# The first products of a two-layer encoder: a new order, small matmuls of zeros ahead of x, and two squares moved back

## The chip, the cores and the metric

The kernel runs on one core of one Trainium2 chip. A core has five engines with a queue each, worked off in order: TensorE (PE in the profile, its weight loads PEld), VectorE (DVE), ScalarE (ACT), GpSimd (POOL) and SyncE (SP, which here only issues transfers). They wait for one another through semaphores. The metric is the device time of one execution in microseconds (us); lower is better.

## The reference

Two layers, each of them: half of a SwiGLU feed-forward, a mixer (convolution, pooling, differential attention), half of a second feed-forward, and a norm. Input and output are 256 tokens of 1024 channels in float32. What is near the change is the start of the first layer:

```python
x = x + 0.5 * swiglu_ffn(rms_norm(x, ffn1_norm[l]), ffn1_w_gate[l], ffn1_w_up[l], ffn1_w_down[l])

def rms_norm(x, g):
    y = xf * lax.rsqrt(jnp.mean(xf * xf, axis=-1, keepdims=True) + NORM_EPS)
    return (y * g.astype(jnp.float32)).astype(x.dtype)

def swiglu_ffn(h, w_gate, w_up, w_down):
    return (jax.nn.silu(h @ w_gate) * (h @ w_up)) @ w_down
```

D_MODEL is 1024 and D_FF is 2816.

## The kernel before

Every matmul of the reference is made of fast single-pass products: each operand is split into a high part (`whi`, rounded by ScalarE) and a low part (`wlo`, the rest, by VectorE), and a product is high by high plus the cross terms. For the feed-forward's first two matrices `mm2` does this with two instructions: 512 columns against the high weights and 256 columns against the low weights. Such a pair is called a pair below.

x stands in four tiles `x[t][c]`: t is the half of the tokens, c the half of the channels, so x00 and x10 hold the first 512 channels and x01 and x11 the second. `Norm.chunk(c)` transposes one half of the channels on TensorE against an identity matrix (it stands in the first 128 columns of `cst`), splits the result into `n0a_xT0` to `n0a_xT3` (or 4 to 7), and sums the squares of x on ScalarE (`n0a_sq`). `Norm.factor` makes the norm's factor of these sums (`n0a_m` on VectorE, `n0a_r` on GpSimd) and spreads it with two TensorE transposes (`n0a_bc`) and a ScalarE copy (`n0a_rbc`). The factor is multiplied in after the products, so products need only the transposed x.

Weights come as 158 pieces of 1 MB through a queue on SyncE: `raw7a` and `raw7b` are the two halves of piece 7, and there are five half-piece buffers. Each piece is split in quarters: `whi7a` to `whi7d` on ScalarE, `wlo7a` to `wlo7d` on VectorE. A half-piece buffer is free when VectorE has made the low parts of it, and only then can SyncE issue the next transfer into it. The first piece comes in four quarters, and x01 and x11 are issued between them. The feed-forward `f0a` uses one piece for each of 22 blocks: block j accumulates the gate product `f0a_g` and the up product `f0a_u` over eight xT in two PSUM banks, of which four are in turn, so block j+2 can begin when ScalarE and VectorE have read block j's banks (`f0a_t`: a copy on ScalarE, then an addition on VectorE).

The order of the instructions is not that of the code. All calls are first recorded as operations with a cost and a lag (`_cost`, in us), and `Program.schedule` plans them: backwards for priorities, forwards to an order, four times, and keeps the shortest plan. `emit` then issues them all from line 429 in that order, so nearly every row of the profile names L429. Costs only set the order: on the chip an engine waits for its semaphores.

The planner prices a float32 matmul like this:

```python
        single = kw["rhs"].tile.dt == F32R
        return (n / 2400 + 0.0135 if single else max(4 * n / 2400 + 0.005, 0.215)), None, 0.0
```

After the first feed-forward has begun, `load_rest` brings the other 1 MB of `cst` through GpSimd's queue, once a buffer is free that TensorE reads.

Of the kernel before, what the change touches and what calls it, by code (L numbers as in the profile page):

```python
# [16 lines left out]
P = 128  # L17
# [38 lines left out]
ROUNDS = 4  # L56
IN_ORDER = ("mm", "raw")
# [152 lines left out]
class Program:  # L210
# [5 lines left out]
    def __init__(self, tc, nc):  # L216
        self.tc, self.nc = tc, nc
        self.ops = []
        self.open = None
        self.chains = {}  # L220
        self.waits = []
        self.after = set()
        for e in ("tensor", "vector", "scalar", "gpsimd", "sync"):
            setattr(self, e, _Engine(self, e))
# [14 lines left out]
    def add(self, engine, call, cost, reads, writes, table, lag):  # L239
        i = len(self.ops)  # L240
        if self.open is None or self.open == "new":
            op = Op()
            op.engine, op.cost, op.calls, op.preds, op.succs, op.tiles = engine, 0.0, [], set(), [], []
            op.table, op.lag = table, lag
            self.ops.append(op)
            if self.open == "new":
                self.open = op
        else:
            op = self.open
            i -= 1  # L250
            assert op.engine == engine
        op.calls.append(call)
# [240 lines left out]
def trunk_kernel(  # L493
# [11 lines left out]
    nc = Program(tc, tc.nc)  # L505
# [43 lines left out]
    cst = cpool.tile([P, P + NH * 384 + 512], F32, tag="cst", name="cst")  # L549
    nc.scalar.dma_start(cst[:, :P], consts[:, :P])  # L550
# [3 lines left out]
    def load_x(c):  # L554
        for t in range(2):
            nc.sync.dma_start(x[t][c], x_in[t * P:(t + 1) * P, c * 512:(c + 1) * 512])
# [22 lines left out]
    upad = cpool.tile([P, 2, SEQ + 2 * PPAD], F32, tag="upad", name="upad")  # L579
    for z in zpad:  # L580
        nc.gpsimd.memset(z, 0.0)
    nc.gpsimd.memset(upad, 0.0)

# [16 lines left out]
    class Norm:  # L600
# [9 lines left out]
        def chunk(self, c):  # L610
            name = self.name
            for kp in range(2):
# [6 lines left out]
                for j in range(2):  # L619
                    k = c * 4 + kp * 2 + j  # L620
                    s = slab_tile(f"{name}_xT{k}")
                    split(s[:, :256], s[:, 256:], tr[:, j * 256:(j + 1) * 256], self.gains[:, k:k + 1])
                    self.xT[k] = (s[:, :256], s[:, 256:])
                    self.xw[k] = s
            for t in range(2):
                sq = tmp.tile([P, 512], F32, tag="sq", name=f"{name}_sq{c}{t}")
                nc.scalar.activation(sq, x[t][c], AF.Square, scale=1.0 / 32.0, accum_out=self.ss[:, t, c:c + 1])
                if self.post is not None:
                    nc.vector.tensor_mul(x[t][c], x[t][c], self.post[:, c * 512:(c + 1) * 512])
                    sq = tmp.tile([P, 512], F32, tag="sq", name=f"{name}_sqg{c}{t}")  # L630
                    nc.scalar.activation(sq, x[t][c], AF.Square, scale=1.0 / 32.0, accum_out=self.ssg[:, t, c:c + 1])

# [348 lines left out]
    for c in range(2):  # L981
        norm.chunk(c)
# [167 lines left out]
```

## Time and profile before

| | us |
|---|---|
| median of three runs | 954.4 |
| the three runs | 954.4, 959.36, 953.64 |
| the profiled execution's own time | 956.96 |
| its span, from the first to the last instruction | 955.2 |

The profiled execution's time is 1.76 us more than its span, which is what lies around the instructions. All times below are from the start of the span. A row of the timeline gives start and duration; matmuls overlap, so the pace of equal neighbours is read from start to start, or from n of them as the duration of the row less that of one, over n - 1. Granted clock is the share of TensorE's 2.4 GHz: 1.00 is that, and 0.50 is 1.2 GHz.

### The profile page before, as it was taken

To read this page: it belongs to the slowest core of one execution; us is meant where nothing else is said; L and a number is where in the kernel's file an instruction comes from. 1 tells how busy PE (TensorE), PEld (TensorE's weight loads), DVE (VectorE), ACT (ScalarE), POOL (GpSimd) and SP (SyncE) were. 2 spreads that over 40 slices of the span, in tenths; PEclk is the share of its full clock that TensorE was granted. 3 is DMA by queue.
4 is the path that set the end of the run, shared out by engine and by line. 5 is a ranking of instruction groups with operands and counts; after the bars stand their busy time and mean duration, and the time that the engine had idled before them with its cause. 6 is when DMAs were issued, how large, how long until landed. Compare 5 with 4: busy or idle time off the path is not lost.

```text
span 955.2 us, 14812 instructions
## 1 busy us (share of the span) xinstructions
PE 934.2 (98%) x5224; PEld 806.7 (84%) x5224; DVE 725.2 (76%) x1500; ACT 587.5 (62%) x1403; POOL 62.4 (7%) x81
## 2 busy tenths in 40 slices
PE   7999999998999999999999999999989999999997
PEld 6888888898878888888888888888988788888885
DVE  6998786659997877776668787755799988777712
ACT  7876665543987666665556666654369776666601
POOL 1000000015220000000000000000321100000000
PEclk9999999998999999999999999999999999999999
DMA  8975568640155655568525555765302755555601
GB/s 299 314 251 189 194 202 284 204 137 24 45 201 180 237 182 191 183 199 294 186 68 197 186 189 196 256 232 181 111 1 90 264 180 194 192 184 185 234 1 45
DMA packets 47915, 171.54 MB, mean 180 GB/s; under 512 B 5344, under 2 KB 5600, under 8 KB 47712
## 3 DMA queue, kind: packets, MB, share of 16 engines
q1 hardware_dynamic: 46656, 167.27, 51.5%
q0 software_dynamic: 608, 2.62, 0.8%
q8 instruction: 41, 0.67, 0.3%
q10 hardware_dynamic: 576, 0.70, 0.2%
q14 instruction: 34, 0.28, 0.1%
HBM read 169.52 MB, written 1.05 MB: 179 GB/s over the span
## 4 chain that ended last, share of the span: by engine, by line
PE 84%; DVE 8%; ACT 3%; DMA 2%; issue 2%; POOL 1%; SPq 0%; POOLq 0%; ACTq 0%
PE f1b_g L429 7%; PE f1b_u L429 7%; PE f0b_u L429 7%; PE f0b_g L429 7%; PE f1a_g L429 6%; PE f1a_u L429 6%; PE f0b_d L429 6%; PE f0a_d L429 6%; PE f1a_d L429 6%; PE f0a_g L429 6%; PE f0a_u L429 5%; PE f1b_d L429 5%; DVE mx_cacc L429 3%; PE mx_qk L429 3%; PE mx_conv L429 2%
## 5 line engine op out<-in xcount | busy, mean ns | idle before, releaser
L429 DVE SCALAR_TENSOR_TENSOR mx_cacc<-zpad,par,mx_cacc 128x256 f32<-128x256 f32 x120 | 56.6, 533 | 0.1
L429 ACT ACTIVATE mx_qksq<-mx_qk 128x64 f32<-128x64 f32 x64 | 13.3, 234 | 19.5 <-PE mx_qk L429 19.5
L429 DVE SCALAR_TENSOR_TENSOR x<-f1b_d,f1b_rh,x 128x512 f32<-128x512 f32 x4 | 3.0, 750 | 29.3 <-PE f1b_d L429 29.3
L429 ACT ACTIVATE fin_sq<-x 128x512 f32<-128x512 f32 x4 | 2.5, 632 | 34.3 <-DVE x L429 34.3
L429 ACT COPY f1a_t<-f1a_g 128x256 f32<-128x256 f32 x22 | 8.2, 373 | 24.7 <-PE f1a_g L429 24.7
L429 POOL DMA_DIRECT2D mx_pwr<-in_pool_w x2 | 1.2, 618 | 315.4 <-PE f1a_d L429 172.0
L429 ACT COPY f1b_t<-f1b_g 128x256 f32<-128x256 f32 x22 | 8.2, 373 | 21.1 <-PE f1b_g L429 21.1
L429 ACT COPY f0b_t<-f0b_g 128x256 f32<-128x256 f32 x22 | 8.2, 373 | 20.6 <-PE f0b_g L429 20.6
L429 ACT COPY f1a_t<-f1a_u 128x256 f32<-128x256 f32 x22 | 8.2, 373 | 18.7 <-PE f1a_u L429 18.7
L429 ACT COPY f1b_t<-f1b_u 128x256 f32<-128x256 f32 x22 | 8.2, 372 | 18.4 <-PE f1b_u L429 18.4
L429 ACT COPY f0a_t<-f0a_g 128x256 f32<-128x256 f32 x22 | 8.2, 373 | 18.0 <-PE f0a_g L429 16.3
L429 ACT COPY f0b_t<-f0b_u 128x256 f32<-128x256 f32 x22 | 8.2, 372 | 17.9 <-PE f0b_u L429 17.9
L429 DVE TENSOR_TENSOR f1a_t<-f1a_t,f1a_u 128x256 f32<-128x256 f32 x22 | 9.3, 421 | 12.4 <-ACT f1a_t L429 12.4
L429 DVE TENSOR_TENSOR f1b_t<-f1b_t,f1b_u 128x256 f32<-128x256 f32 x22 | 9.2, 419 | 12.2 <-ACT f1b_t L429 12.2
L429 DVE TENSOR_TENSOR f0b_t<-f0b_t,f0b_u 128x256 f32<-128x256 f32 x22 | 9.2, 420 | 11.7 <-ACT f0b_t L429 11.7
L429 DVE TENSOR_TENSOR f1b_t<-f1b_t,f1b_g 128x256 f32<-128x256 f32 x22 | 9.2, 420 | 10.9 <-ACT f1b_t L429 10.9
L429 DVE TENSOR_TENSOR f0b_t<-f0b_t,f0b_g 128x256 f32<-128x256 f32 x22 | 9.3, 421 | 10.7 <-ACT f0b_t L429 10.7
L429 POOL TENSOR_TENSOR mx_qkf<-mx_qkf,mhalf 128x8 f32<-128x8 f32 x8 | 14.6, 1827 | 39.8 <-DVE mx_qkf L429 39.8
L429 ACT ACTIVATE mx_e<-mx_e,mx_mx 128x256 f32<-128x256 f32 x32 | 16.0, 504 | 1.1 <-DVE mx_mx L429 1.0
L429 DVE TENSOR_TENSOR f1a_t<-f1a_t,f1a_g 128x256 f32<-128x256 f32 x22 | 9.2, 420 | 9.6 <-ACT f1a_t L429 9.6
L429 ACT ACT_TABLE_LOAD x12 | 15.4, 1283 | 1.9 <-PEq L1141 1.7
L429 ACT COPY f0a_t<-f0a_u 128x256 f32<-128x256 f32 x22 | 8.2, 373 | 13.2 <-PE f0a_u L429 13.0
(4003 smaller groups left out, 3909.2 us busy)
## 6 DMA issues: line engine op xcount, KB each, us to landing
x<-in_x SPq DMA_DIRECT2D x4, 256.0 KB, 5.0
cst<-in_consts POOLq DMA_DIRECT2D x1, 1024.0 KB, 9.8
post<-in_post_rows POOLq DMA_DIRECT2D x2, 512.0 KB, 4.3
raw0a<-in_weights SPq DMA_DIRECT2D x2, 256.0 KB, 5.1
raw0b<-in_weights SPq DMA_DIRECT2D x2, 256.0 KB, 5.7
raw1a<-in_weights SPq DMA_DIRECT2D x1, 512.0 KB, 6.3
raw1b<-in_weights SPq DMA_DIRECT2D x1, 512.0 KB, 7.2
raw2a<-in_weights SPq DMA_DIRECT2D x1, 512.0 KB, 8.0
```

Source lines behind the costliest of these rows:

```text
L429: getattr(getattr(self.nc, engine), method)(*[a.resolve() if isinstance(a, View) else a for a in args], **{k: a.resolve() if isinstance(a, ...
```

## The change

There are four edits.

First, `nc.slow` gives the next recorded operation an extra cost and lag in the planner's account: 0.5 of lag for the identity's transfer, 0.75 and 1.0 of cost for the transfers of x00 and x10, and 0.85 of cost for the first clearing of `zpad`. This changes no instruction, only the planned order.

Second, 26 matmuls of 64 columns are recorded behind the clearing of `zpad`. They multiply zeros of `zpad0` by zeros into a PSUM bank of their own that nothing reads.

Third, `chunk` takes a flag; for the first norm of the kernel it makes the squares of x01 and x11 wait in the plan until xT7 is made.

Fourth, the planner turns all this into a new order.

```diff
+WARM = 26
...
+        self.slow = (0.0, 0.0)
...
+        cost += self.slow[0]
+        op.lag += self.slow[1]
+        self.slow = (0.0, 0.0)
...
+    nc.slow = (0.0, 0.5)
     nc.scalar.dma_start(cst[:, :P], consts[:, :P])
...
         for t in range(2):
+            if c == 0:
+                nc.slow = (0.75, 1.0)[t], 0.0
             nc.sync.dma_start(x[t][c], x_in[t * P:(t + 1) * P, c * 512:(c + 1) * 512])
...
+    nc.slow = (0.85, 0.0)
     for z in zpad:
         nc.gpsimd.memset(z, 0.0)
     nc.gpsimd.memset(upad, 0.0)
+
+    warm = bank("warm")
+    for _ in range(WARM):
+        nc.tensor.matmul(warm[:, :64], lhsT=zpad[0][:, :P], rhs=zpad[0][:, :64], start=True, stop=True)
...
-        def chunk(self, c):
+        def chunk(self, c, late=False):
...
+            if late and c == 1:
+                nc.waits = [self.xw[7]]
             for t in range(2):
                 sq = tmp.tile([P, 512], F32, tag="sq", name=f"{name}_sq{c}{t}")
                 nc.scalar.activation(sq, x[t][c], AF.Square, scale=1.0 / 32.0, accum_out=self.ss[:, t, c:c + 1])
...
+            nc.waits = []
...
-        norm.chunk(c)
+        norm.chunk(c, True)
```

The order differs only near the start: in the first 80 rows of TensorE, the first 105 or so of VectorE and ScalarE, and by one exchange on GpSimd (`zpad0` is cleared ahead of a constant). SyncE's order, and so that of all weights and of x, is the same.

TensorE's first rows before, from the first transposes of x to the first product (`n0a_tr00` and `n0a_tr01` are the PSUM banks of the first half's transposes, `n0a_tr10` and `n0a_tr11` those of the second):

```order
L429 MATMUL n0a_tr00_102<-cst_75,x00_79 128x128 x2
L429 MATMUL n0a_tr01_105<-cst_75,x00_79 128x128 x2
L429 MATMUL n0a_tr00_102<-cst_75,x10_87 128x128 x2
L429 MATMUL n0a_tr01_105<-cst_75,x10_87 128x128 x2
L429 MATMUL n0a_tr10_139<-cst_75,x01_97 128x128
L429 MATMUL n0a_tr11_143<-cst_75,x01_97 128x128
...
L429 MATMUL f0a_g0_149<-n0a_xT0_123,whi0a_126 128x512
```

The same place after the change:

```order
L435 MATMUL warm_87<-zpad0_77 128x64 x12
L435 MATMUL n0a_tr00_116<-cst_75,x00_79 128x128
L435 MATMUL n0a_tr01_119<-cst_75,x00_79 128x128
L435 MATMUL warm_87<-zpad0_77 128x64
...
L435 MATMUL warm_87<-zpad0_77 128x64 x6
L435 MATMUL n0a_tr00_116<-cst_75,x10_89 128x128 x2
L435 MATMUL n0a_tr01_119<-cst_75,x10_89 128x128 x2
L435 MATMUL warm_87<-zpad0_77 128x64 x7
L435 MATMUL n0a_tr10_166<-cst_75,x01_129 128x128
...
L435 MATMUL f0a_g0_178<-n0a_xT0_143,whi0a_148 128x512
```

Twelve matmuls of zeros now stand ahead of the first transpose, seven ahead of those of x10 and seven ahead of those of x01; all 26 stand ahead of the first product.

ScalarE before, from the second weight quarter to the second piece:

```order
L429 CAST whi0c_134<-raw0b_95 128x512
L429 ACTIVATE n0a_sq10_141,n0a_ss_100<-x01_97 128x512
L429 ACTIVATE n0a_xT2_152<-n0a_tr01_105,par_85 128x256
L429 ACTIVATE n0a_sq11_156,n0a_ss_100<-x11_111 128x512
L429 ACTIVATE n0a_xT3_168<-n0a_tr01_105,par_85 128x256
L429 CAST whi0b_174<-raw0a_93 128x512
L429 ACTIVATE n0a_xT4_181<-n0a_tr10_139,par_85 128x256
```

ScalarE after the change, at the same place and on to the squares:

```order
L435 CAST whi0c_160<-raw0b_121 128x512
L435 ACTIVATE n0a_xT2_168<-n0a_tr01_119,par_81 128x256
L435 ACTIVATE n0a_xT3_176<-n0a_tr01_119,par_81 128x256
L435 ACTIVATE n0a_xT4_186<-n0a_tr10_166,par_81 128x256
...
L435 CAST whi1b_234<-raw1a_163 128x512
L435 ACTIVATE n0a_sq10_242,n0a_ss_114<-x01_129 128x512
L435 CAST whi1c_250<-raw1b_192 128x512
L435 ACTIVATE n0a_sq11_257,n0a_ss_114<-x11_134 128x512
L435 CAST whi1d_265<-raw1b_192 128x512
```

The two squares moved from among the splits of x to among the casts of the second piece, behind all eight xT; with them `n0a_m`, `n0a_r` and `n0a_bc` come later, and the copy `n0a_rbc` now stands directly ahead of block 0's copy.

## Rows read from the trace of the kernel before

**Rows 1.** The page, part 1: busy time of each engine, share, instructions.

```profile
PE 934.2 (98%) x5224; PEld 806.7 (84%) x5224; DVE 725.2 (76%) x1500; ACT 587.5 (62%) x1403; POOL 62.4 (7%) x81
```

**Rows 2.** The chain that ended last, 0 to 40 us: start, length, what.

```profile
8.30 1.11 PE n0a_tr L429 x4
9.41 0.64 PE f0a_g L429 x2
10.05 0.85 PE n0a_tr L429 x4
...
12.82 0.53 PE f0a_g L429 x2
...
16.01 1.73 PE f0a_g L429 x10
```

**Rows 3.** Stretches of 2 us: busy time by engine, then granted clock, DMA share, GB/s.

```profile
10.00:12.00 2.00, 2.00 (x10) 1.81 (x9) 1.66 (x5) 1.84 (x5) 0.71 (x1) 1.00 0.97 373
...
226.00:228.00 2.00, 0.00 (x0) 0.00 (x0) 2.00 (x6) 0.34 (x4) 2.00 (x2) 1.00 0.01 4
...
230.00:232.00 2.00, 2.00 (x12) 2.00 (x11) 2.00 (x6) 0.84 (x6) 0.00 (x0) 0.50 0.00 0
...
236.00:238.00 2.00, 2.00 (x19) 1.73 (x18) 2.00 (x7) 0.98 (x10) 1.73 (x1) 1.00 0.00 0
```

**Rows 4.** Timeline of all engines, 0 to 12 us; in brackets idle time and its releaser.

```profile
0.78 0.61 POOL L429 MEMSET zpad<- 128x286 f32 x2
...
3.90 1.11 PE L429 MATMUL n0a_tr<-cst,x 128*128 128x128 f32 x4 [3.90 <-DMA cst<-in_consts]
...
5.46 1.12 PE L429 MATMUL n0a_tr<-cst,x 128*128 128x128 f32 x4 [0.45 <-DMA x<-in_x]
...
6.19 0.47 ACT L429 ACTIVATE n0a_xT<-n0a_tr,par 128x256 fp32r<-128x256 f32 x1
...
8.34 0.63 ACT L429 ACTIVATE n0a_sq<-x 128x512 f32<-128x512 f32 x1
```

**Rows 5.** Timeline of PE in the mixers: transposes, and float32 matmuls of 2 columns.

```profile
270.81 0.38 PE L429 MATMUL mx_aT<-cst,mx_e 128*128 128x128 f32 x2
...
738.67 1.02 PE L429 MATMUL mx_o<-mean_v,mx_osb 128*128 128x2 f32 x7
```

**Rows 6.** Two tiles: their weight loads, duration in ns min/median/max, first and last start.

```profile
L429 PEld LDWEIGHTS n0a_tr<-cst,x x16: 179/228/231, 3.9 to 10.3; 128*128 128x128 f32 x16
...
L429 PEld LDWEIGHTS mx_o<-mean_v,mx_osb x32: 186/190/192, 267.6 to 746.4; 128*128 128x128 f32 x32
```

**Rows 7.** Timeline of DVE and ACT, 12 to 24 us.

```profile
12.62 0.88 DVE L429 SCALAR_TENSOR_TENSOR n0a_xT<-n0a_tr,par,n0a_xT 128x256 fp32r<-128x256 f32 x2
...
21.24 0.37 ACT L429 COPY f0a_t<-f0a_g 128x256 f32<-128x256 f32 x1 [2.14 <-PE f0a_g L429]
...
21.65 0.42 DVE L429 TENSOR_TENSOR f0a_t<-f0a_t,f0a_g 128x256 f32<-128x256 f32 x1 [1.39 <-ACT f0a_t L429]
```

**Rows 8.** The chain that ended last, 30 to 43 us.

```profile
32.09 0.60 DVE wlo6d L429
...
37.14 5.64 DMA raw10a<-in_weights
```

**Rows 9.** Timeline by engine, 44 to 46 us: DVE, then PE.

```profile
44.72 0.42 DVE L429 TENSOR_TENSOR f0a_t<-f0a_t,f0a_g 128x256 f32<-128x256 f32 x1
...
44.85 0.28 PE L429 MATMUL f0a_u<-n0a_xT,wlo5d 128*128 128x256 f32 x1
45.19 0.50 PE L429 MATMUL f0a_g<-n0a_xT,whi6a 128*128 128x512 f32 x1
```

**Rows 10.** Timeline of POOL near 42 us, and that transfer's median us to landing.

```profile
41.94 0.54 POOL L429 DMA_DIRECT2D cst<-in_consts  x1
...
cst<-in_consts POOLq DMA_DIRECT2D x1, 1024.0 KB, 9.8
```

**Rows 11.** A stretch of 5 us: busy time of PE, PEld, DVE, ACT, POOL, clock, DMA.

```profile
30.00:35.00 5.00, 5.00 (x31) 4.39 (x30) 5.00 (x12) 4.64 (x9) 0.00 (x0) 1.00 0.88 279
```

## The prediction

> **What bounds the kernel now.** I read the page first: TensorE is busy 98% of the span [rows 1], so a change at the start pays only by letting TensorE do its work earlier, and only if nothing later takes the time back. Next the chain that ended last. From 8.30 us on it is TensorE alone: four transposes, a pair, four transposes, then pairs [rows 2]. TensorE does not idle there; it is slow. A pair at 9.41 takes 0.64 us, the one at 12.82 takes 0.53, and five pairs at 16.01 take 1.73, so 0.346 each [rows 2]. The ratio of 0.64 to 0.346 is that of the two clock levels, 1.2 and 2.4 GHz. The column of granted clock reads 1.00 at 10 to 12 us already [rows 3], but ten matmuls in 2 us there stand against full pace later; the column seems to have no entry for the start. Where it has one, the picture is the same: TensorE stands idle at 226 to 228, is granted 0.50 at 230 to 232, and has 1.00 again at 236 to 238 [rows 3]. So TensorE starts at 1.2 GHz and comes to 2.4 some 4.5 us after its steady work begins at 8.30; in the mixer it took between 6 and 8 us.
>
> Then I followed the first wait behind the start. At 45.19 the gate product of block 6 starts, 0.34 us after the last matmul of block 5 where 0.11 to 0.12 is the pace, so TensorE lost 0.22 us [rows 9]. It waited for a PSUM bank that VectorE's addition at 44.72 sets free [rows 9], and that addition stands behind the splits of piece 10, whose transfer was issued at 37.14 and took 5.64 us [rows 8]. From 16 us to there TensorE has no other gap on the chain. This spot is the second gate that a gain must pass.
>
> **The change part by part.** *The planner's extra costs* put no instruction on the chip and cost nothing by themselves; they act through the order.
>
> *The clock.* The work from 8.30 to 13.35 is 8 transposes (1.11 and 0.85 us) and 5 pairs (four of 0.64, one of 0.53), together 5.05 us [rows 2]. At full clock two transposes take 0.38 us [rows 5], of which one by itself is 0.27, so the pace is 0.11 us, and a pair 0.346, so 8 x 0.11 + 5 x 0.346 = 2.61 us. If the zeros bring the clock up before 8.30, TensorE gains 5.05 - 2.61 = 2.4 us. That is the ceiling of this part; its floor is 0, if the zeros do not count as work.
>
> *The 26 matmuls of zeros.* The first waits for the clearing of zpad0. Two clearings took 0.61 us from 0.78 [rows 4]; with zpad0 first, TensorE starts at about 1.15 us. No row shows a 64-column float32 matmul. The nearest rows: a 2-column float32 matmul of the program is two records (32 for 16), and seven of them take 1.02 us [rows 5], one by itself 0.25, so the pace is (1.02 - 0.25)/6 = 0.13 with small gaps and 0.11 without, hence 0.22 to 0.26 per matmul at full clock. At half clock four 128-column transposes take 1.11 us [rows 4], one by itself 0.42, a pace of 0.23 against 0.11 at full, which would make 0.43 to 0.46 of two records if the weight load sets the pace. But a load that stands alone takes as long at half clock as at full, 179 and 186 ns [rows 6], so the doubling may be that of 128 moving columns, and 64 of them would hide behind the load. I take 0.22 at either clock and keep 0.46 as the other end.
>
> With 0.22 the first twelve end at 1.15 + 2.64 = 3.8 us, before the identity lands at 3.90, and cost nothing. Four transposes (0.9) and seven more (1.54) end at 6.35 at half clock, where x10's transposes could start at 5.46 [rows 4]. What is queued behind is the split of xT0 on ScalarE, at 6.19 before [rows 4]: it moves to about 6.9, and VectorE's chain with it. Then 0.45 to 0.9 for four transposes and 1.54 for the last seven: x01's transposes come at 8.3 to 8.8 against 8.30 before. So the zeros cost TensorE 0 to 0.5 us; I take 0, since the clock should rise at 1.15 + 4.5 = 5.7 to 1.15 + 7 = 8.2.
>
> The page "TensorE: Matmul & The Clock Gate" of the Trainium skill, section "What's actually happening", says that the gate's timing runs freely and does not start anew with a kernel, so that one kernel sees its clock rise at different points in different runs. The two rises of this trace, 4.5 and 6 to 8 us after work began, agree with that. By it the gain of a run would scatter between the ceiling and what a rise at 8.2 leaves.
>
> *The squares.* Two operations of 0.63 us [rows 4] leave the place between the splits of x and go behind them. The path of the splits gets shorter by that, ScalarE's total does not. Behind the moved squares hang the norm's sum, its power on GpSimd, the two spreading transposes and a ScalarE copy that now stands directly before block 0's copy. TensorE reaches the first spreading transpose behind 24 pairs and 8 transposes, 8.30 + 0.9 + 8.3 = 17.5 us; ScalarE has until then done eight splits, two squares and seven casts since 6.9. Eight at 0.47, two at 0.8 and seven at 0.62 would be 9.7 us if nothing overlapped, so 16.6 at the latest. A margin of about 1 us hides it. Without that cover TensorE would wait out the difference.
>
> *What this makes at 45 us.* Before, VectorE idled 1.39 us until block 0's first addition at 21.65, because ScalarE's copy at 21.24 waited 2.14 us for TensorE [rows 7]. From then on it has hardly a gap (5.00 of 5 us at 30 to 35 [rows 11]), and it is VectorE's pace that frees the half-piece buffers and issues piece 10. So the chain to 45.19 moves by as much as that addition moves. After the change, VectorE has eight splits of xT at 0.44 (two take 0.88 [rows 7]) and fourteen low parts at 0.60 [rows 8] before it: 3.5 + 8.4 = 11.9 us from 7.4 on, so 19.3, and 0.5 to 1 us of waits for the cast behind the first moved square: 19.8 to 20.3. TensorE completes block 0 as the 28th pair, at 8.30 + 0.9 + 28 x 0.346 = 18.9 us, and a copy of 0.37 follows, so VectorE is later. The addition comes 1.35 to 1.85 us earlier; I take 1.4. TensorE itself arrives 2.4 us earlier and was held 0.22 before, so VectorE decides: 1.4 us are kept.
>
> *The 1 MB through GpSimd's queue.* It is issued at 41.94 and takes 9.8 us to land [rows 10], so it hardly touched piece 10, landed at 42.78 [rows 8]. Its issue waits for a buffer that TensorE frees, so it moves by 2.4 us and piece 10 by only 1.4: they overlap for about 1.9 us. 1 MB in 9.8 us is 107 GB/s, a third of the 279 to 373 GB/s of these stretches [rows 3, 11]; a third of 1.9 is 0.6 us at most, 0 if queues did not share. I take 0.2.
>
> The page "DMA: Bandwidth & Descriptors" of the Trainium skill, section "Issuing engines are not separate DMA queues", says that transfers of all issuing engines end up on the same 16 DMA engines and interleave. By that the 0.6 would be paid and the gain would be 0.8; with separate queues it would be 1.4. No row of this trace tells the two apart at this spot.
>
> The sum: 1.4 - 0.2 = 1.2 us less. The profiled execution would go from 956.96 to 955.8 us. It stands 2.6 above the median of the three runs, 954.4, with the same order of instructions, so I forecast the median by the same step: 954.4 - 1.2 = **953.2 us**. Behind 45 us nothing else is reordered, and waits in the mixers are between engines that all move together.
>
> **The rivals.** *Piece 10 does not move* (time as before): if transfers, not VectorE, set its landing, TensorE wins 2.4 us at the start and waits 2.4 at 45. DMA share is 0.97 early and 0.88 at 30 to 35 [rows 3, 11], close to full, which speaks for it; that VectorE is full in the same stretch speaks against. Time: 954.4, with 0.5 either way.
>
> *The zeros hold up x* (slower): at 0.43 a matmul and with a clock that they don't lift, the zeros and the first 8 transposes end at 1.15 + 26 x 0.43 + 8 x 0.23 = 14.2 us instead of 8.30. If the clock then rises at 13 as before, the last 1.2 us of that shrink to 0.6, and what follows runs at full speed, which saves the 2.4: 14.2 - 8.30 - 0.6 - 2.4 = 2.9 us late, 957.3. It decides from the pace at which zeros and transposes fill the time to 8.30: (8.30 - 1.15 - 1.84)/26 = 0.20 if the clock stays low. At 0.22 this is already passed by 0.4 us, so this rival needs both: no lift, and the slow pace.
>
> *All of it is kept* (faster still): if the addition of block 4 lands early enough, 2.4 us remain: 952.0. Against it stands the count of VectorE's work above.
>
> *The change does nothing* to the clock at all but costs no time: within 0.5 of 954.4, counted with the first rival.
>
> **How the numbers follow.** Forecast 0.50 (952.3 to 954.0), piece 10 or no effect 0.25 (953.9 to 954.9), zeros hold up x 0.17 (954.8 to 957.3, and 960 at the worst), all kept 0.08 (952.0). Runs of one kernel differ here by 5.7 us at the most and by 0.8 between the nearer two, so a median can lie half a microsecond off. The range takes in all but the outer part of the slow rival: 951.6 to 956.4. A change of 1% would be 9.5 us, and about that much is what a measurement of this kernel tells from no change; none of these cases reaches it. Faster by over 1%: 0.01, slower: 0.01, the same: 0.98.
>
> **What would show it.** In the profile after, pairs of 0.35 us from the first product on confirm the clock; pairs of 0.64 deny it. The first transposes at 3.9 and x10's before 6.4 confirm the price of the zeros; first transposes at 6 us speak for 0.43. Block 0's first addition at 20 to 20.5 and piece 10's transfer issued at about 35.7 confirm the shift; block 6 then starts at about 44.0 behind a wait of about 1 us. If it starts at 45.2, the first rival holds. A clock that rises and falls again before the products would make me wrong, as would a mixer whose slow stretch, 228 to 236, gets longer or shorter by chance: at half clock each us there costs half.

## Result and profile after

| | us |
|---|---|
| after, median of five runs | 964.21 (960.38 to 966.36) |
| before, median of five runs beside them | 955.66 (953.64 to 959.36) |
| ratio | 1.0079, 95% interval 1.0058 to 1.0100 |
| after, profiled execution: time, span | 966.36, 964.6 |

The forecast was 953.2, with a range of 951.6 to 956.4. The change is slower: by 0.8%, that is 7.5 us, with 5.5 to 9.6 by the interval; the two medians are 8.6 us apart. The median lies 7.8 us above the upper end of the range. The page of the profile says that TensorE is still busy 98% of the span, the same share as in [rows 1]: the time did not go into idling. Part 1 of the page after:

```profile
PE 947.1 (98%) x5276; PEld 817.8 (85%) x5276; DVE 724.5 (75%) x1500; ACT 586.1 (61%) x1403; POOL 62.4 (6%) x81
```

These are 52 more records (26 matmuls of two records each) and 12.9 us more of busy time. The timeline of TensorE after, 0 to 20 us:

```profile
1.11 5.38 PE L435 MATMUL warm<-zpad 128*128 128x64 f32 x24 [1.11 <-POOL mhalf L435]
6.29 0.63 PE L435 MATMUL n0a_tr<-cst,x 128*128 128x128 f32 x2
...
7.46 2.66 PE L435 MATMUL warm<-zpad 128*128 128x64 f32 x12
9.91 1.06 PE L435 MATMUL n0a_tr<-cst,x 128*128 128x128 f32 x4
10.77 3.09 PE L435 MATMUL warm<-zpad 128*128 128x64 f32 x14
13.65 1.17 PE L435 MATMUL n0a_tr<-cst,x 128*128 128x128 f32 x4
14.46 0.78 PE L435 MATMUL f0a_g<-n0a_xT,whi0a 128*128 128x512 f32 x1
...
16.75 0.63 PE L435 MATMUL f0a_g<-n0a_xT,whi0a 128*128 128x512 f32 x1
...
18.84 0.39 PE L435 MATMUL f0a_g<-n0a_xT,whi0a 128*128 128x512 f32 x1
```

Read from start to start, the first 24 records take (6.29 - 1.11)/24 = 0.216 us each and the last 14 take 0.206, so a matmul of zeros costs 0.41 to 0.43 us and not 0.22. The transposes of x00, x10 and x01, at 3.90, 5.46 and 8.30 in [rows 2, 4], stand at 6.29, 9.91 and 13.65. A product of 512 columns still takes 0.63 at 16.75 and 0.39 only at 18.84: after 13 us of work without a gap on zeros and transposes TensorE is at 1.2 GHz, and it comes to 2.4 only about 4 us into the products, as before. The first product is 5.4 us late (14.46 against 9.06).

What else is late. ScalarE's timeline after, then SyncE's:

```profile
12.49 0.84 ACT L435 ACTIVATE n0a_xT<-n0a_tr,par 128x256 fp32r<-128x256 f32 x2
15.92 0.84 ACT L435 ACTIVATE n0a_xT<-n0a_tr,par 128x256 fp32r<-128x256 f32 x2 [2.59 <-PE n0a_tr L435]
16.64 0.62 ACT L435 CAST whi0b<-raw0a 128x512 fp32r<-128x512 f32 x1
```

```profile
6.22 0.48 SPq L435 DMA_DIRECT2D raw2a<-in_weights  x1
18.29 0.33 SPq L435 DMA_DIRECT2D raw2b<-in_weights  x1
```

In the new order the cast `whi0b` stands behind the splits xT4 and xT5, and these wait for x01's transposes behind the zeros. `wlo0b` follows, and only it frees the half-piece buffer into which raw2b goes. So SyncE issues no transfer of weights between 6.22 and 18.29 us (before, raw2b was issued at 11.71). Stretches of 5 us after, columns as in [rows 3]:

```profile
10.00:15.00 5.00, 5.00 (x24) 4.80 (x24) 3.08 (x6) 2.70 (x6) 0.00 (x0) 1.00 0.57 229
15.00:20.00 5.00, 5.00 (x23) 4.47 (x22) 3.21 (x7) 4.08 (x10) 0.00 (x0) 1.00 0.14 52
...
50.00:55.00 5.00, 3.15 (x12) 2.45 (x12) 5.00 (x12) 3.88 (x10) 0.01 (x1) 0.74 1.03 399
```

The DMA share, 0.97 at 10 to 12 us in [rows 3], is 0.57 and then 0.14. The transfers behind that are issued late: raw2b by 6.6 us, raw6b to raw8b by 5.6, raw9a to raw10b by 6.3. At block 6 TensorE waits. What it waited for there (total, times, longest), and the chain of waits after:

```profile
PE f0a_g L435 <- DVE f0a_t L435: 1.8, 1, 1.8
```

```profile
26.90 0.37 ACT f0a_t L435
...
31.35 5.39 DMA raw6b<-in_weights
...
42.27 6.07 DMA raw9b<-in_weights
...
51.82 0.42 DVE f0a_t L435
52.24 0.04 issue
52.28 4.63 PE f0a_g L435 x16
56.91 2.82 PE f0a_u L435 x16
...
332.50 2.77 PE f0b_g L435 x16
```

It is the spot of [rows 9], with the same addition behind the splits of piece 10, but TensorE idles 1.8 us there; by starts it loses 2.0 (52.28 behind 50.16) instead of 0.22.

The stretch without transfers is not on this chain. From 1.13 to 26.88 us the chain is TensorE alone, and ScalarE's copy of block 0 waits for it, 5.7 us later than before (26.90 against 21.24 in [rows 7]). The issue of raw6b comes late by as much, 5.6. Two transfers on the chain then took longer than before: raw6b 5.39 us against 4.51, raw9b 6.07 against 5.03. In the 18 traces of this study raw6b takes 4.0 to 5.6 us and raw9b 4.1 to 6.9, so these times may belong to the execution and not to the change. That the late casts cause the wait at block 6 is not shown.

In this execution the clock fell behind that wait as well: granted clock 0.74 in 50 to 55, and 4.63 us for 16 records that take 2.82 right after. By starts, TensorE is 5.4 us late at the first product, 5.3 at the end of block 5, 7.1 at block 6, 8.7 at its up product (56.91 against 48.24), 10.3 at the first down product, and between 7.3 and 10.3 from there to the end. What moves in that last span is told with the two paces below, and so is the last row.

### The profile page after: what moved, and what is told of

The parts are those of the page before. It is cut to its first block, busy times and chain, and to the rows that moved or that the text cites. A ratio compares the mean times of both kernels' runs of the same rounds, so it can differ in the third digit from the quotient of the medians.

```text
span 964.6 us, 14918 instructions
## 1 busy us (share of the span) xinstructions
PE 947.1 (98%) x5276; PEld 817.8 (85%) x5276; DVE 724.5 (75%) x1500; ACT 586.1 (61%) x1403; POOL 62.4 (6%) x81
## 4 chain that ended last, share of the span: by engine, by line
PE 86%; DVE 7%; DMA 3%; ACT 2%; issue 2%; POOL 0%; POOLq 0%; ACTq 0%; SPq 0%; DVEq 0%
PE f1b_g L435 6%; PE f1a_g L435 6%; PE f1b_u L435 6%; PE f1a_u L435 6%; PE f0b_g L435 6%; PE f0b_u L435 6%; PE f0a_d L435 6%; PE f1a_d L435 6%; PE f0b_d L435 6%; PE f0a_g L435 5%; PE f0a_u L435 5%; PE f1b_d L435 5%; DVE mx_cacc L435 3%; PE mx_qk L435 2%; PE mx_conv L435 2%; PE mx_v L435 2%
## 5 line engine op out<-in xcount | busy, mean ns | idle before, releaser
L435 ACT ACTIVATE mx_qksq<-mx_qk 128x64 f32<-128x64 f32 x64 | 13.3, 233 | 19.1 <-PE mx_qk L435 19.1
L435 DVE TENSOR_TENSOR f1b_t<-f1b_t,f1b_g 128x256 f32<-128x256 f32 x22 | 9.2, 420 | 11.3 <-ACT f1b_t L435 11.3
```

Of the source, the lines that this page charges most:

```text
L435: getattr(getattr(self.nc, engine), method)(*[a.resolve() if isinstance(a, View) else a for a in args], **{k: a.resolve() if isinstance(a, ...
```

## Experiments

All starts below are from traces, one execution for each label, in us from the start of its span. The wait is TensorE's idle time at block 6 for VectorE's addition; none means under 0.1 us. By starts, before, before_again and no_zeros each lose 0.20 to 0.23 us there all the same. The paces are those of a pair in the four feed-forwards, from starts over 16 pairs, in ns; for the first it is that behind block 6.

| kernel | first product | raw2b issued | block 6 | wait | first down product | paces | span |
|---|---|---|---|---|---|---|---|
| before | 9.06 | 11.71 | 45.19 | none | 134.05 | 347 353 347 353 | 955.2 |
| before_again | 8.59 | 11.40 | 45.53 | none | 136.09 | 353 347 353 353 | 956.2 |
| no_zeros | 8.82 | 12.65 | 45.68 | none | 134.53 | 347 347 353 353 | 953.3 |
| zeros6 | 9.02 | 12.85 | 45.13 | 0.6 | 135.68 | 353 353 353 353 | 958.2 |
| zeros_alone | 11.37 | 13.84 | 47.36 | 0.9 | 137.92 | 353 353 347 353 | 957.4 |
| zeros_alone_again | 12.76 | 13.84 | 48.82 | none | 137.67 | 347 347 347 353 | 956.3 |
| two_cols | 14.37 | 18.19 | 52.02 | 1.3 | 142.58 | 353 347 353 353 | 961.1 |
| ones | 14.46 | 18.29 | 51.71 | 1.7 | 142.26 | 353 347 353 353 | 961.8 |
| after | 14.46 | 18.29 | 52.28 | 1.8 | 144.37 | 353 347 353 353 | 964.6 |
| after_again | 14.46 | 18.29 | 51.30 | 0.6 | 141.85 | 353 353 353 353 | 963.2 |
| dense14 | 8.71 | 11.94 | 44.95 | 1.1 | 135.50 | 353 353 353 353 | 957.3 |
| dense14_lag4 | 8.30 | 12.01 | 42.81 | none | 131.56 | 347 347 353 353 | 951.8 |
| dense14_lag4_again | 9.23 | 13.16 | 44.52 | none | 134.97 | 353 347 353 353 | 952.8 |
| before_lag4 | 9.24 | 11.87 | 44.27 | none | 133.02 | 347 347 353 353 | 952.7 |
| after_lag4 | 14.81 | 18.86 | 50.40 | none | 139.15 | 347 353 353 353 | 960.2 |
| after_wlag | 14.36 | 17.92 | 49.70 | none | 140.16 | 353 347 353 353 | 960.7 |
| dense14_wlag | 9.33 | 12.65 | 44.40 | none | 133.15 | 347 347 353 353 | 953.0 |
| before_wlag | 9.49 | 12.12 | 45.95 | none | 136.41 | 353 347 347 353 | 952.5 |

Timed runs (medians; "before" is the kernel before on the same chip in the same hour):

| kernel | us | before | ratio, 95% interval |
|---|---|---|---|
| no_zeros | 957.12 | 956.89 | 1.0010, 0.9995 to 1.0026 |
| dense14 | 957.54 | 956.89 | 1.0013, 0.9997 to 1.0028 |
| zeros_alone | 959.83 | 956.86 | 1.0031, 1.0011 to 1.0051 |
| dense14_lag4 | 955.08 | 956.86 | 0.9986, 0.9971 to 1.0001 |
| before_lag4 | 955.28 | 956.86 | 0.9979, 0.9961 to 0.9997 |
| zeros6 | 958.33 | 956.89 | 1.0013, 1.0000 to 1.0027 |
| after_lag4 | 962.23 | 956.89 | 1.0049, 1.0032 to 1.0066 |
| after_wlag | 961.93 | 957.92 | 1.0037, 1.0025 to 1.0050 |
| dense14_wlag | 955.73 | 957.92 | 0.9982, 0.9969 to 0.9995 |
| before_wlag | 953.45 | 957.92 | 0.9956, 0.9939 to 0.9972 |

The other labels have one execution each: two_cols 962.88, ones 963.57, after_again 965.04, before_again 957.96, zeros_alone_again 958.08, dense14_lag4_again 954.57.

The theory: the zeros are paced by their weight loads at the low clock, do not raise it, and hold up x; the rest follows from the late splits. The first rival: the new order and the late squares do it.

**Without the zeros (no_zeros).**

```diff
-WARM = 26
-    warm = bank("warm")
-    for _ in range(WARM):
-        nc.tensor.matmul(warm[:, :64], lhsT=zpad[0][:, :P], rhs=zpad[0][:, :64], start=True, stop=True)
```

> The change without its 26 matmuls of zeros: planner costs, the order that follows, and the late squares stay. Theory 1 (the zeros alone hold up the start, and the empty weights queue behind it makes the wait at block 6): first product near 9.1 to 9.4 us as before, clock up near 13, block 6 near 45.2 us, no second stretch at half clock near 52, time within 1 us of the kernel before. Theory 2 (the new order and the late squares make the wait at block 6): first product near 9.4, but block 6 still waits 1 us or more and the clock falls there again; 3 us or more slower than before.

TensorE's timeline of no_zeros:

```profile
8.82 0.78 PE L433 MATMUL f0a_g<-n0a_xT,whi0a 128*128 128x512 f32 x1
...
45.35 0.28 PE L433 MATMUL f0a_u<-n0a_xT,wlo5d 128*128 128x256 f32 x1
45.68 0.49 PE L433 MATMUL f0a_g<-n0a_xT,whi6a 128*128 128x512 f32 x1
```

The first product is at 8.82. Block 6 is at 45.68 and loses 0.22 us by starts, as in the kernel before. The ratio is 1.0010 with an interval that takes in 1. The order and the late squares by themselves cost nothing that can be measured; they move raw2b by 0.9 us and block 6 by 0.5. The rival falls, as long as there are no zeros.

**What paces the zeros (two_cols, ones).** In two_cols the 26 matmuls have 2 columns; in ones `zpad0` holds ones until they are done.

```diff
-        nc.tensor.matmul(warm[:, :64], lhsT=zpad[0][:, :P], rhs=zpad[0][:, :64], start=True, stop=True)
+        nc.tensor.matmul(warm[:, :2], lhsT=zpad[0][:, :P], rhs=zpad[0][:, :2], start=True, stop=True)
```

```diff
-    for z in zpad:
-        nc.gpsimd.memset(z, 0.0)
+    nc.gpsimd.memset(zpad[0], 1.0)
+    nc.gpsimd.memset(zpad[1], 0.0)
...
+    nc.gpsimd.memset(zpad[0], 0.0)
```

> The changed kernel with matmuls of zeros of 2 columns instead of 64, same order. Theory 1 (the weight load sets their pace): 0.44 to 0.45 us a matmul as with 64, first product at 14.2 to 14.8, time as after the change. Rival (the moving columns set the pace): under 0.30 a matmul, first product before 11.5, 3 us or more faster than after.

> The changed kernel with the same 26 matmuls in the same places, but of ones by ones (zpad0 is filled with 1 first and cleared behind them). Theory 1 (matmuls of 64 columns behind a weight load each leave the clock low whatever the data): 0.45 us each, pairs of 0.64 after the first product at 14.5, clock up near 18. Rival (zeros do not count because they are zeros): the clock rises while they run, later ones take 0.22 to 0.26, first product before 12 with pairs of 0.35.

TensorE's timeline of two_cols, then of ones:

```profile
1.11 5.28 PE L435 MATMUL warm<-zpad 128*128 128x2 f32 x24 [1.11 <-POOL zpad L435]
6.25 0.67 PE L435 MATMUL n0a_tr<-cst,x 128*128 128x128 f32 x2
```

```profile
1.11 5.38 PE L435 MATMUL warm<-zpad 128*128 128x64 f32 x24 [1.11 <-POOL mhalf L435]
...
16.74 0.63 PE L435 MATMUL f0a_g<-n0a_xT,whi0a 128*128 128x512 f32 x1
17.17 0.39 PE L435 MATMUL f0a_g<-n0a_xT,wlo0a 128*128 128x256 f32 x1
17.38 0.40 PE L435 MATMUL f0a_u<-n0a_xT,whi0c 128*128 128x512 f32 x1
```

With 2 columns a record takes (6.25 - 1.11)/24 = 0.214 us, as with 64: the moving columns do not pace it. What both have in common is a weight load of 128 columns for each record, which is the pace that is left; no run changed the load by itself. With ones the start is the same to 0.01 us, at the low clock to 17.2: that the data are zeros is not the reason.

**Six zeros (zeros6).**

```diff
-WARM = 26
+WARM = 6
```

> The changed kernel with 6 matmuls of zeros instead of 26, all ahead of the first transposes. Theory 1 (0.45 us each, and what fits in before the identity lands costs nothing): they end at 3.8 us, first transposes near 3.9, first product at 8.8 to 9.4 us, clock up at 11 to 14 as without them, no wait over 0.5 us at block 6, time within 1.5 us of the kernel before. Rival (other parts of the change cost): 959 or more.

```profile
1.11 2.83 PE L435 MATMUL warm<-zpad 128*128 128x64 f32 x12 [1.11 <-POOL mhalf L435]
3.93 1.12 PE L435 MATMUL n0a_tr<-cst,x 128*128 128x128 f32 x4
```

This is TensorE's timeline: the six end at 3.94, just as the identity lands, and x is not held up. The ratio is 1.0013 with an interval from 1.0000 to 1.0027, and the medians are 1.4 us apart: within 1.5, as expected. The wait at block 6 was 0.6, a little over the bound given.

**Zeros alone, twice.** The kernel before with the 26 matmuls recorded behind its clearing of `zpad`; 23 stand ahead of the first product, and the squares and `whi0b` stay where they were on ScalarE.

```diff
     nc.gpsimd.memset(upad, 0.0)
+    warm = bank("warm")
+    for _ in range(26):
+        nc.tensor.matmul(warm[:, :64], lhsT=zpad[0][:, :P], rhs=zpad[0][:, :64], start=True, stop=True)
```

> The kernel before with the 26 matmuls of zeros alone, without the planner's extra costs and with the squares in their old place; 23 of the 26 stand ahead of the first product. Theory 1 (zeros hold up the start and with it the queue of weights): 0.45 us each, first product at 12.5 to 13.5, raw2b issued 4 to 6 us later than before, a wait of 1 us or more at block 6, 5 to 9 us slower than before. Theory 2 (the wait at block 6 comes of the late squares and the new order): wait there at most 0.5 us, 3.5 to 4.5 us slower.

> The kernel before with the 26 matmuls of zeros alone, once more; last time the clock rose while zeros ran, at 9.8 us. Theory A (the point of the rise differs between runs): another point this time, anywhere from 9 to 16 us. Theory B (this order of zeros and transposes lifts it): again within 0.3 us of 9.8.

TensorE's timeline of the first run, then of the second:

```profile
8.74 2.65 PE L429 MATMUL warm<-zpad 128*128 128x64 f32 x18
...
11.37 0.47 PE L429 MATMUL f0a_g<-n0a_xT,whi0a 128*128 128x512 f32 x1
```

```profile
8.74 3.94 PE L429 MATMUL warm<-zpad 128*128 128x64 f32 x18
...
12.76 0.78 PE L429 MATMUL f0a_g<-n0a_xT,whi0a 128*128 128x512 f32 x1
...
17.04 0.56 PE L429 MATMUL warm<-zpad 128*128 128x64 f32 x4
```

To 8.74 us the two runs agree within 0.01. Then the same 18 records take 2.65 us once and 3.94 the other time: in the first run the clock rose while they ran, in the second only after the first product. So one kernel can have its rise at different points, and once it did come during such matmuls. The record notes different chips for the two runs, so this pair does not tell the run from the chip. In the other seven traces that have 23 or 26 of them ahead (after, after_again, ones, two_cols, after_lag4, after_wlag and this second run) it came behind the first product. What raised it in that one run stays open. The page "TensorE: Matmul & The Clock Gate" of the Trainium skill, section "What's actually happening", says that the gate's timing runs free of the kernel's start; these two traces agree. At full clock four records take 0.56 at 17.04, so 0.11 each, and 0.21 at the low one: the pace of these records follows the clock. The section "LDWEIGHTS (loading the stationary operand)" of the same page prices a load by its columns alone; by its formula, 128 columns are an estimate of 107 ns. That fits the 0.11 us at the full clock here, and at the low one the measured 0.21 decides.

The expected 5 to 9 us did not come: 1.0031, or 3.0 us by medians. Much of the difference to the change lies at the first product already: it is 2.3 and 3.7 us later than before in these two traces, and 5.4 in the change. A loss of 3.0 us is what that alone would give. The second difference is raw2b: 13.84 in both runs, against 18.29. With `whi0b` ahead of xT4 (12.48 us on ScalarE, against 16.64) the weights go on although x is late, so the new order makes the zeros' delay the weights' delay. That this costs time is not shown: the wait at block 6 does not follow raw2b. At 13.84 it is 0.9 us once and none the other time, at 11.94 (dense14, below) it is 1.1, and at 18.86 (after_lag4, below) there is none.

**Dense zeros (dense14).** 14 single-pass matmuls of 512 columns from a tile that VectorE clears; 8 ahead of the first transposes, then 3 and 3.

```diff
+    zw = slab_tile("zw")
+    nc.vector.memset(zw.bitcast(F32), 0.0)
     for _ in range(WARM):
+        nc.slow = (0.2, 0.0)
-        nc.tensor.matmul(warm[:, :64], lhsT=zpad[0][:, :P], rhs=zpad[0][:, :64], start=True, stop=True)
+        nc.tensor.matmul(warm, lhsT=zw[:, :P], rhs=zw, start=True, stop=True)
```

> The changed kernel with 14 single-pass matmuls of zeros of 512 columns in place of the 26 of 64 columns in float32, cleared by VectorE; 8 ahead of the first transposes, 3 and 3 behind. Theory 1 (dense columns lift the clock, zeros or not): 0.43 us each from about 1.2 us, 0.22 after the clock rises between 4 and 8 us; first product at 9.1 to 10 and pairs of 0.35 from there; block 0 done 1 to 2.4 us earlier than before, of which block 6 keeps 0 to 1.4; time 0 to 1.5 us under the kernel before. Rival (zeros do not count): 0.43 throughout, first product near 10, pairs of 0.64 until 13 to 14, 1 to 2 us slower than before.

TensorE's timeline, then the chain of waits, both of dense14:

```profile
1.44 3.49 PE L435 MATMUL warm<-zw 128*128 128x512 f32 x8 [1.44 <-DVE zw L435]
...
5.12 0.94 PE L435 MATMUL warm<-zw 128*128 128x512 f32 x3
...
8.71 0.48 PE L435 MATMUL f0a_g<-n0a_xT,whi0a 128*128 128x512 f32 x1
...
9.92 0.40 PE L435 MATMUL f0a_g<-n0a_xT,whi0a 128*128 128x512 f32 x1
...
10.27 0.39 PE L435 MATMUL f0a_u<-n0a_xT,whi0c 128*128 128x512 f32 x1
...
44.95 0.51 PE L435 MATMUL f0a_g<-n0a_xT,whi6a 128*128 128x512 f32 x1 [1.06 <-DVE f0a_t L435]
```

```profile
36.19 6.34 DMA raw10a<-in_weights
...
44.48 0.42 DVE f0a_t L435
```

Eight take 3.32 us from start to start, 0.415 each; three later ones 0.94, so 0.23 each. In all four traces with 14 matmuls of 512 columns the clock was up ahead of the first product, though they multiply zeros. They differ from the small ones in two things, the columns and the kind (single-pass against float32 of two records), and no run parts these. The pairs run at 0.35 from 9.92, and TensorE leads the kernel before by 2.4 us at 11.3: the ceiling of the prediction, to a tenth. At block 6 the lead is 0.24. Piece 10's transfer was issued 0.95 us earlier than in [rows 8], but it took 6.34 us instead of 5.64 and landed at 42.53 against 42.78. Of the 2.4 us, 1.3 are left at the last pair of block 5 (43.36 against 44.62). The two spreading transposes, which this order has later, took 0.24, a first wait at block 2 for block 0's addition took 0.5, and pairs of 353 ns against 347 the rest. The wait of 1.06 at block 6 took 1.0 more, and the total is the same within what was measured.

**The addition ahead of the splits (lag4).** The planner is told that a transfer lands later, and then puts block 4's first addition ahead of the splits of pieces 9 and 10. This is not its only effect: by the traces, before_lag4 and before differ in 245 places of TensorE's order, all behind 180 us, at the ends of the feed-forwards and in the mixers, and VectorE's and ScalarE's orders differ from 18 to 20 us on.

```diff
-    return 0.05 + 128 * n * 4 / 360e3, None, 2.2
+    return 0.05 + 128 * n * 4 / 360e3, None, 4.0
```

> The kernel with 14 dense matmuls of zeros, and the planner told that a transfer on SyncE's queue lands 4.0 us after its cost instead of 2.2; this puts block 4's first addition ahead of the splits of pieces 9 and 10 on VectorE. Theory 1 (the gain of the start is given back at block 6 because that addition stands behind the splits of piece 10): block 6 starts near 42.8 to 43.3 us without a wait, the lead of 2 us is still there at 60 us, and the time is 1 to 2.5 us under the kernel with 14 dense matmuls. Rival (the weights' transfers themselves are late): TensorE waits 1 us or more at another block before 60 us and nothing is kept.

> The kernel with 14 dense matmuls of zeros and 4.0 us, once more. The start does not depend on the run if dense zeros lift the clock: rise between 4 and 7 us, first product near 8.3 to 9, block 6 within 0.5 us of 42.8 without a wait, pairs of 347 ns in the first feed-forward. The other feed-forwards may have either pace, 2.3 us each, so the span lies between 949.5 and 957.

> The kernel before with the planner's 4.0 us in place of 2.2 and nothing else. Theory 1: block 6 starts 0.2 us earlier since it waited only 0.22 there, time within 0.5 us of the kernel before, unless the new order does something else in the mixers. Rival (the new order is itself worth something): 1.5 us or more off, in either direction.

> The changed kernel with the planner's 4.0 us in place of 2.2, which puts block 4's first addition ahead of the splits of pieces 9 and 10; all 26 matmuls of zeros still stand ahead of the first product (21, then 5). Theory 1 (the zeros cost 5.4 us at the start, and the wait at block 6 with the slow pairs behind it 2 to 5 us more): first product at 14.5 to 15 if the clock stays low, no wait at block 6, pairs of 347 ns in the first feed-forward from there, time 960 to 962, so 2.5 to 4.5 us under the change. Rival (the late weights make TensorE wait wherever the addition stands): a wait of 1 us or more at another block of the first ten, and 963 to 965 as after the change.

VectorE's timeline of dense14_lag4, then TensorE's:

```profile
39.76 0.42 DVE L435 TENSOR_TENSOR f0a_t<-f0a_t,f0a_g 128x256 f32<-128x256 f32 x1
...
41.03 0.69 DVE L435 TENSOR_TENSOR wlo9a<-raw9a,whi9a 128x512 fp32r<-128x512 f32 x1
...
43.77 0.69 DVE L435 TENSOR_TENSOR wlo10a<-raw10a,whi10a 128x512 fp32r<-128x512 f32 x1
```

```profile
42.69 0.28 PE L435 MATMUL f0a_u<-n0a_xT,wlo5d 128*128 128x256 f32 x1
42.81 0.39 PE L435 MATMUL f0a_g<-n0a_xT,whi6a 128*128 128x512 f32 x1
```

The addition now starts at 39.76, ahead of the splits. Block 6 starts 0.12 us behind block 5, at 42.81, 2.4 earlier than before, and the first down product is 2.5 earlier. In none of the seven traces with such an order (lag4, and wlag below) does TensorE wait at block 6, so the wait there is shown to come of the addition's place. In the second run the clock rose later (the first twelve dense matmuls took 5.49 us instead of 4.34), the pace was 353 from the first block on, and block 6 came at 44.52, outside of what was expected. By the timed runs, dense14_lag4 and before_lag4 cannot be told apart (955.08, 955.28). The order itself is worth something to the kernel before, too: 1.6 us by medians, 0.3 to 3.7 by the interval, where at most 0.5 had been expected. As it changes more than block 6, this gain is not put down to one place.

In after_lag4 the wait is gone and the pairs keep 347; the ratio is 1.0049. But before_lag4 gained as well, and after_lag4 is still 7.0 us over it by medians, so this does not say that the wait was what was regained.

**The same for pieces 1 to 157 alone (wlag).** The first piece keeps its lag. The start does not keep its order, though. Apart from the zeros, after_wlag has TensorE's first 34 records in the order of the change; then the squares and the spreading transposes come earlier (`n0a_bc` at 21.13 against 25.08). dense14_wlag and before_wlag also part early from dense14 and before, and all three have the later differences of lag4.

```diff
+            self.nc.slow = (0.0, 1.8)
             self.nc.sync.dma_start(raw[h], self.src[i, :, h * 1024:(h + 1) * 1024])
```

> The changed kernel with 1.8 us more lag in the plan for the transfers of pieces 1 to 157 only, so that the start with its zeros stays as it is and block 4's first addition stands ahead of the splits of piece 9. Theory 1 (beyond the start the loss is the wait at block 6 and the slow pairs behind it): first product at 14.4 to 14.5, block 6 near 50.0 to 50.7 without a wait over 0.3 us, pairs of 347 ns from there in the first feed-forward, time 960 to 962.3. Rival (it is something else): 963 or more.

> The kernel with 14 dense matmuls of zeros (8, 3 and 3) and the same 1.8 us of lag. Theory 1 (the lead of the start is kept when block 6 does not wait): first product 8.3 to 8.8 with pairs of 0.35, block 6 at 42.6 to 43.3, time 1 to 2.4 us under the kernel before with the same lag, if both have the same mix of pair paces. Rival (something later takes it): block 6 early, but no more than 0.5 us under that kernel, and the first product of the down stage no earlier.

> The kernel before with the 1.8 us of lag and nothing else. Block 6 at 44.2 to 45.0 without a wait, time 0 to 1.5 us under the kernel before.

after_wlag has no wait at block 6 and lands in the expected time, 961.93, but its pairs run at 353 from the first block on, which was not expected. Against before_wlag it is still 8.5 us slower. So the loss by medians is as large without the wait as with it. By the traces of the two, TensorE is 4.9 us late at the first product and 3.8 at block 6 and at the first down product; the rest comes behind, 2.2 of it in the third feed-forward, which ran at 353 in one trace and 347 in the other, and 1.2 and 1.0 in the stretches around the two mixers, told below.

dense14_wlag was expected under before_wlag and is 2.3 us over it, by medians of 11 and 5 runs. In the traces it leads by 3.3 us at the first down product (133.15 against 136.41), 2.3 of which is pace, and is 0.5 behind at the end (953.0 against 952.5). The traces show where the lead goes: 2.2 in the third feed-forward's pace, 0.3 and 0.9 in the stretches around the two mixers, 0.4 in the second feed-forward. Why these differ is open. before_wlag is the fastest kernel of the study by medians, 0.44% under the kernel before, where at most 1.5 us had been expected (its block 6 came at 45.95, later than expected, with pairs at 353). From the first down product of the third feed-forward to the first product of the fourth it takes 157.0 us, against 159.2 in both traces of the kernel before. This stretch around the second mixer takes 157.0 to 159.2 in the seven traces with a lag4 or wlag order and 158.5 to 160.2 in the other eleven, so that order, which differs there, may have a part in it. But in the two traces of dense14_lag4, one kernel, it takes 159.2 and 157.0, so one trace of each kernel does not show it. The same stretch around the first mixer takes 157.6 to 160.2.

**The same kernels once more.**

> The changed kernel once more. Theory 3 (the pace of the pairs, 347 or 353 ns, is set at a gap of TensorE and held to the end of that feed-forward): again only these two levels, each held from a gap on; where the gaps and the clock's falls are different, which feed-forwards have which level may be different too. Rival (the level belongs to the kernel): again slow, fast, slow, slow from block 6 on.

> The kernel before once more. If the pace of the pairs belongs to the run and not to the kernel, at least one feed-forward has the other pace than in the first trace (347, 353, 347, 353 ns); the last has had 353 in every trace so far and should have it again. The clock rises anywhere from 2 to 5 us after the first product at 9.1.

The chain of waits of after_again, in the second feed-forward; the row of after there is the last one of its chain above:

```profile
332.45 2.83 PE f0b_u L435 x16
```

One kernel, the same instructions, TensorE without a gap, and eight pairs take 2.83 us here and 2.77 there. In the 18 traces each feed-forward keeps one of the two paces from its first blocks to its end, apart from the first, where it can turn at block 6: six traces have 347 ns ahead of a wait of 0.6 us or more there, and all six 353 behind it. It turned the other way once, in no_zeros, from 353 to 347. A wait is not needed: four others ran at 353 in the first feed-forward without it. 352 pairs at 6.6 ns more are 2.3 us, about as much as the whole gain under study. The last feed-forward had 353 in all 18. The chip is a rival that these pairs do not settle: for zeros_alone and dense14_lag4 the record notes another chip for the second trace, and for the first traces of before and after it notes none. The timed runs of the kernel before, on one chip each, spread over 4.6 to 7.4 us, so much of the spread is there without a change of chip.

## Why the prediction was wrong, step by step

- **"I take 0.22 at either clock and keep 0.46 as the other end."** This step failed. It rested on a load that stands alone, 179 and 186 ns at either clock [rows 6], and took that for its pace in a row of loads. The measured pace is 0.21 a record at the low clock with 64 columns and with 2, so 0.41 to 0.43 a matmul. The nearer row, transposes at 0.23 against 0.11 [rows 4, 5], was the right one, and [rows 6] has the median of the loads at the low clock as 228 ns. 26 times 0.2 is 5.2 us more than priced, and the first product is 5.4 late. The planner has nearly the same price, 0.215 us at any clock, so it put twelve ahead of the first transposes, where six fit (zeros6).
- **"I take 0, since the clock should rise at 1.15 + 4.5 = 5.7 to 1.15 + 7 = 8.2."** This failed as well, and for the same matmuls: in the two traces of the change, and in ones and two_cols, it rose behind 16.7 us, only after products had begun. The 4.5 us "after its steady work begins" of the prediction had been counted from transposes and products of up to 512 columns, and was carried over to matmuls of 64 columns without a row of them.
- **The ceiling of 2.4 us** was right: dense zeros reach it, though it lasts only to block 2.
- **The spot at 45 us** was seen rightly, but "1.4 are kept" was not: dense14 kept 0.24. Block 0's addition moved up by 1.1 us (20.54 against 21.65) where 1.4 were forecast, the transfer's issue by 0.95, and then the transfer itself took 0.7 us longer. This is the outcome of the rival in which piece 10 does not move, but only in part its mechanism: the issue did follow VectorE. The transfer takes 4.9 to 6.9 us in the 18 traces, so the 0.7 may be chance.
- **The rival "zeros hold up x"** is what happened, at 13.65 where it counted 14.2. It gave 957.3, and 960 at worst, because it credited a clock that rises at 13 all the same, 3.0 us; the clock rose with the products, so nothing came back. And it stopped at TensorE: it did not ask what is queued behind the late splits. `whi0b` behind xT4 on ScalarE stops the weights' queue for 12.1 us, 5.3 before. That SyncE's order is the same was true, and its times were not; what this costs is not shown.
- **The squares** cost nothing that can be measured (no_zeros), as forecast. The transfer of 1 MB on GpSimd's queue was not tried by itself, so its term of 0.2 us is neither shown nor refuted.
- **"Behind 45 us nothing else is reordered"** was right for TensorE. VectorE's and ScalarE's orders differ from those before up to 59 and 57 us; no_zeros and zeros6 have the change's order there too and are 0.2 and 1.4 us over the kernel before by medians. Times behind that differ from trace to trace, by 2.3 us a feed-forward with its pace and by up to 3.1 us in the stretch around a mixer.

Of the 7.5 us (5.5 to 9.6), then, 5.4 are shown at the first product and go with the zeros (no_zeros). The wait at block 6 was 0.6 to 1.8 us in the four traces that have all 26 zeros ahead and the old place of the addition, and the pairs behind it were slow in all four, worth up to 1.7 over the 16 blocks from there. But without the wait the loss is no smaller beyond doubt: after_lag4 is 7.0 us over before_lag4, and after_wlag 8.5 over before_wlag. And the second traces of the two kernels part by 5.9 us at the first product (14.46 against 8.59), 5.8 at the first down product and 7.1 at the end, where the pace of the second feed-forward makes 2.3 of it. So what is left beyond the first product is about as large as what paces and mixers differ by from trace to trace, and its cause stays open.

## What to carry to other kernels

Price an operation that fills a gap at the clock that the gap has, and by its pace in a row, not by one instance; six of these fillers fitted, 26 did not. A filler meant to raise the clock has to be tried for that: with the single-pass matmuls of 512 columns the clock was up ahead of the first product in four traces of four, with 23 or 26 of the small float32 ones in one of eight. Then look at the first spot behind, where a buffer or a bank comes free: a lead that stops there is worth nothing. When an engine's order is changed, ask which casts or copies that feed another queue now stand behind a wait, and then follow the chain to see whether that costs anything: here a queue that stood still for 12 us was not on it. Before a difference of 2 us between two traces is put down to a change, compare them stretch by stretch, and with a second trace of the same kernel.

## What the hardware showed beyond that

- The pairs have two paces at full clock, 347 and 353 ns, each held for a feed-forward; which one differs between traces of one kernel. What sets it is open.
- The clock's rise varies between two traces of one kernel: in zeros_alone it came between 8.7 and 11.2 us, and in its second run between 13.3 and 15.1.
- The clock fell behind the wait of 1.8 us at block 6 in one trace of the change; behind waits of 1.7 and 1.3 in ones and two_cols it did not.
- Transfers that are issued earlier need not land as much earlier: in dense14, 0.95 us of lead at the issue of piece 10 became 0.25 at its landing [rows 8]. The same half-piece takes 4.9 to 6.9 us in the 18 traces.
